# A two-layer hybrid decoder on one core: transposing attention probabilities six units behind their scores instead of four, with the second embedding kept in DRAM

## The chip, the cores and the metric

The kernel runs on one core of one Trainium2 chip. The metric is the device time of an execution in microseconds (us). Before the change the median of three runs is 1397.23 us, the lowest 1396.04, the highest 1397.76.

## What is computed

A decoder of two layers over 512 tokens of width 1024. Layer 0 mixes by retention and mLSTM heads, layer 1 by sparse attention with 16 query heads in two groups; in both a gated MLP with a short convolution and a gated input embedding follow. The change lies in layer 1: its attention, and the embedding that is computed beside the attention and used in the MLP behind it.

```
def reference(...):                                    # layer i = 1
    h = h + nsa_mixer(rms_norm(h, nsa_norm_g), ...)    # sparse attention
    h = h + conv_ffn(rms_norm(h, ffn_norm_g[i]), ...)  # gelu(conv(a)) * b, then down
    e = rms_norm(p[i] @ ple_w[i], ple_norm_g[i])       # the input embedding
    gate = sigmoid(rms_norm(h, ple_gate_norm_g[i]) @ ple_w_gate[i])
    h = h + gate * e

# in nsa_mixer, for each block of 128 queries:
    s = einsum('bghqd,bgnd->bghqn', qq, kc) * scale    # compressed keys: 31 of them
    p_c = softmax(where(cvalid, s, NEG));  o_cmp = p_c @ vc
    ...                                                # selected and window branch:
    p_s = softmax(where(smask, s, NEG));   o_slc = p_s @ vg
    p_w = softmax(where(wmask, s, NEG));   o_win = p_w @ vwb
    return g[..., 0:1] * o_cmp + g[..., 1:2] * o_slc + g[..., 2:3] * o_win
```

With 512 tokens all eight blocks of 64 are selected and the window of 512 covers everything, so both branches are causal attention over all keys, each with its own keys and values.

## The kernel before

Activations lie transposed, features on the partitions and the 512 tokens along the free axis. Each large product runs as three matmuls of split numbers (`mm3`, L152 to L154): high times high, high times low, low times high. A weight tile of 512 KB is loaded by SP (`load`, L146), copied to its high half by ACT (L133) and its remainder made by DVE or POOL (L134; `lo_seq` says which of the two); three tiles are in flight.

**Attention.** The work is cut in 96 units, six for each head: `UNITS` names the query block j (3, 1, 2, 0) and the branches b of each unit. The blocks j = 3 and j = 2 are too wide for both branches in a PSUM bank and take two units, the others one. A loop written out by hand (L1046 and on, `for step in range(...)`) does in each step: `scores` of unit `step`; `probs` of unit `step - LAG`; the hooks of that step; `values` of the heads that are due. The `values` of half a head come `VALUES_LAG` steps behind the last transposes that they read.

- `scores` (L889 to L910): two matmuls of queries with keys (L899, L900) and one that adds the causal mask (L901), into one of four PSUM banks "a"; DVE takes the negative maximum (L902), ACT the exponential with its sum (L904). When both branches of a block are there, DVE takes the reciprocal of the sums (L907) and POOL multiplies each branch by reciprocal and gate (L909), in place. The exponential goes to a tile "pr" of 128 x 512, of which there are six.
- `probs` (L912 to L923): PE transposes the gated probabilities in blocks of 128 x 128 (L921) into one of three PSUM banks "b"; ACT and DVE split them into high (L133) and low half (L134), tiles "pt".
- `values` (L925 and on): the products with the compressed values (L931, L932) and with the values (L943) into the one bank "o"; ACT (L947), DVE (L951) and POOL (L134) add and split the head's result.

**Hooks.** Beside the units, at steps given in `START`, stand the eight steps of the embedding (steps 1 to 8), the norm of the second group's queries (L818 to L831, steps 6 and 14), their transposes (L838, from 20), the second group's compressed scores and probabilities (L858 to L880, steps 42 and 47), the fetch of four blocks of the residual that had been kept in DRAM (L103, step 51), and the eight pieces of the first half of the output projection (`out_piece`, steps 60 to 74). The second half of the projection follows the loop and ends with L277.

**The embedding** (`Embed`, from L1116 on). `step(m)` computes rows 128 m and on, and ACT copies them out of PSUM (L1132) to where `place(m)` says. For layer 1 that is a tile of the pool "y", 28 tiles of 128 x 512 that also hold the split normed input, the split queries, the compressed probabilities and the split head outputs. `later(i)` is called in the MLP behind each pair of up products: it squares and sums the eight tiles, then scales them.

The program's order is the order of priority; a scheduler puts the instructions on each engine and gives out the tiles, and weight loads carry a priority 500 instructions ahead (`AHEAD`). So on PE transposes of one unit stand between scores of others. Each engine, SP's queue of DMAs too, works through its own list in order.

Of the kernel before, what the change touches and what calls it, by code (L numbers as in the profile page):

```python
# [10 lines left out]
F32 = mybir.dt.float32  # L11
# [8 lines left out]
P = 128  # L20
T = 512
NTT = T // P
D = 1024
KD = D // P
# [5 lines left out]
OFF = (0, 512, 1024, 896)  # L30
SPAN = 1280
WARM = 10
LAG, VALUES_LAG = 4, 2
UNITS = ((3, (0,)), (3, (1,)), (1, (0, 1)), (2, (0,)), (2, (1,)), (0, (0, 1)))
START = {"embed": (1, 1), "q_norm": (6, 8), "q_stack": (20, 6), "cmp_scores": 42, "cmp_probs": 47, "fetch": 51, "out": (60, 2)}
BANKS = {"a": 4, "b": 3, "o": 1}
# [15 lines left out]
class Norm:  # L52
    def __init__(self):
        self.h, self.l = [], []


class Rows(list):
    pass


class Trunk:
# [553 lines left out]
    def nsa_mixer(self):  # L615
        nc, I, tc = self.nc, self.I, self.tc
# [3 lines left out]
        with ExitStack() as ctx:  # L620
            np_ = ctx.enter_context(tc.tile_pool(name="nsa", bufs=1))
# [262 lines left out]
                return pc  # L884


            parts = []

            def scores(hd, j, bs):  # L889
                g, nb = hd // 8, len(bs)  # L890
                w = (j + 1) * P
                qt, br = qs[hd][:, j * P : w], slice(bs[0], bs[-1] + 1)
                nmx = np_.tile([P, nb], F32, name=self.nm("nmx"), tag=f"sm{nb}", bufs=4)
                if bs[0] == 0:
                    parts.append([np_.tile([P, 2], F32, name=self.nm("sm"), tag="sums", bufs=4), []])
                sm, prs = parts[-1]
                pr = np_.tile([P, T], F32, name=self.nm("pr"), tag="pr", bufs=6)[:, 0 : nb * w].rearrange("p (b s) -> p b s", b=nb)
                s = self.ps("a")[:, 0 : nb * w].rearrange("p (b s) -> p b s", b=nb)
                nc.tensor.matmul(s, qt, kst[0][g][:, br, 0:w], start=True, stop=False)  # L899
                nc.tensor.matmul(s, qt, kst[1][g][:, br, 0:w], start=False, stop=False)  # L900
                nc.tensor.matmul(s[:, :, j * P : w], identb, maskb.unsqueeze(1).to_broadcast([P, nb, P]), start=False, stop=True)  # L901
                nc.vector.tensor_reduce(nmx, s, AX, ALU.max, negate=True)  # L902
                for b in range(nb):
                    nc.scalar.activation(pr[:, b], s[:, b], AF.Exp, bias=nmx[:, b : b + 1], accum_out=sm[:, bs[b] : bs[b] + 1])  # L904
                    prs.append(pr[:, b])
                if bs[-1] == 1:
                    nc.vector.reciprocal(sm, sm)  # L907
                    for b in range(2):
                        nc.gpsimd.tensor_scalar(prs[b], prs[b], sm[:, b : b + 1], gate[:, j, hd, 1 + b : 2 + b], ALU.mult, ALU.mult)  # L909
                return pr  # L910
# [93 lines left out]
            def piece(half, m):  # L1004
                return lambda: self.out_piece(I["w_nso"], half, m, *outs[half])

            emb = self.Embed(self, 1, lambda m: self.y().bitcast(F32))

            def embed(m):
                def run():  # L1010
# [54 lines left out]
    def ffn(self, i, e):  # L1065
        nc, I, tc = self.nc, self.I, self.tc
        with ExitStack() as ctx:
# [4 lines left out]
            def mm_up(f):  # L1072
                self.cycle = ("a", "b")
                return self.ws(I["w_up"][i, f], n), self.ws(I["w_up"][i, NF + f], n)
# [25 lines left out]
                    nc.vector.tensor_tensor(self.h[m], self.h[m], ps, ALU.add)  # L1100

            first = mm_up(0)
            self.norm_scale(n)
            act_up(0, *first)
            part = 0
# [8 lines left out]


    class Embed:  # L1116
        def __init__(self, trunk, i, place):
            self.k, self.i, self.place = trunk, i, place
            self.n, self.e = Norm(), []

        def step(self, m):
            tr, nc = self.k, self.k.nc
            if m == 0:
                self.p = [x.rearrange("p (k t) -> p k t", k=2) for x in tr.load(tr.I["pT"][self.i])]
            if m % 4 == 0:
                self.w = tr.load(tr.I["w_ple"][self.i, m // 4])
            ps = tr.bank()
            for k in range(2):
                s = slice(((m % 4) * 2 + k) * P, ((m % 4) * 2 + k + 1) * P)
                tr.mm3(ps, self.w[0][:, s], self.w[1][:, s], self.p[0][:, k], self.p[1][:, k], k == 0, k == 1)  # L1130
            e = self.place(m)
            nc.scalar.activation(e, ps, AF.Copy)  # L1132
            self.e.append(e)

        def later(self, i):
            tr = self.k
            if i < KD:
                tr.acc_square(self.n, i, self.e[i])
            elif i == KD:
                tr.norm_scale(self.n)  # L1140
            elif i <= 2 * KD:
                e = self.e[i - KD - 1]
                tr.nc.gpsimd.tensor_tensor(e, e, self.n.b, ALU.mult)
# [138 lines left out]
```

## Time and profile before

| | |
|---|---|
| median of three runs | 1397.23 us |
| the profiled execution, its own time | 1398.08 us |
| its span, first to last instruction | 1396.3 us |
| PE busy | 1369.7 us, 98% |
| DVE busy | 850.2 us, 61% |
| ACT busy | 638.8 us, 46% |
| POOL busy | 348.8 us, 25% |
| read from HBM, written | 122.60 MB, 3.15 MB |

The profile is of one execution. An engine counts as busy while an instruction of its own runs; waiting and issuing are not busy. Matmuls overlap and their ends are modelled, so a short pause of PE can hide behind the end of the matmul before it. The attention of layer 1 goes from about 764 us to 966 us; there DVE and ACT are far busier than in the mean over the span.

### The profile page before, as it was taken

How to read it: one execution, taken by the hardware profiler on the slowest of the kernel's cores; microseconds unless marked ns; L12 is line 12 of the kernel's file. 1: busy time of each engine (PE TensorE's matmuls, PEld its weight loads, DVE VectorE, ACT ScalarE, POOL GpSimd, SP SyncE). 2: the span in 40 equal slices, each digit the busy share in tenths (PEclk: the TensorE clock that was granted, in tenths of full speed). 3: DMA queues.
4: the chain of work that ended last, by engine and by line, in shares of the span. 5: the costliest groups of instructions: out<-in, count | busy, mean ns of one | idle time of the engine just before them, and what ended most of it. 6: DMA issues, size and time to landing. Idle time of an engine off the chain costs nothing.

```text
span 1396.3 us, 17997 instructions
## 1 busy us (share of the span) xinstructions
PE 1369.7 (98%) x6726; PEld 1123.2 (80%) x6726; DVE 850.2 (61%) x1382; ACT 638.8 (46%) x1121; POOL 348.8 (25%) x347
## 2 busy tenths in 40 slices
PE   9999999999999999999999899999999999999998
PEld 7778778888888888887788677777888888888887
DVE  6665656666356434566857898776566346534555
ACT  5257426444124323454455787676444223313441
POOL 4466101132031101122110765544122023100120
PEclk9999999999999999999999999999999999999999
DMA  6433323232323323233343100010233323333232
GB/s 216 123 113 105 107 77 104 91 106 91 106 85 98 105 91 97 84 124 103 107 143 98 46 1 31 29 33 21 87 105 94 102 76 108 104 91 102 80 106 76
DMA packets 40031, 127.96 MB, mean 92 GB/s; under 512 B 4740, under 2 KB 5380, under 8 KB 39944
## 3 DMA queue, kind: packets, MB, share of 16 engines
q1 hardware_dynamic: 39656, 126.68, 29.4%
q8 instruction: 53, 0.87, 0.3%
q14 instruction: 34, 0.28, 0.1%
q10 hardware_dynamic: 288, 0.14, 0.0%
HBM read 122.60 MB, written 3.15 MB: 90 GB/s over the span
## 4 chain that ended last, share of the span: by engine, by line
PE 82%; DVE 4%; issue 4%; ACT 4%; POOL 2%; DMA 0%; POOLq 0%; DVEq 0%; ACTq 0%
PE ps L152 25%; PE ps L153 25%; PE ps L154 25%; PE ps L943 2%; PE ps L921 1%; ACT pr L904 1%; DVE nmx L902 1%; ACT pt L133 1%; DVE wl L134 1%; PE ps L363 1%; DVE pt L134 1%; PE ps L899 1%; PE ps L900 1%; PE ps L421 1%; POOL acc L200 1%
## 5 line engine op out<-in xcount | busy, mean ns | idle before, releaser
L152 PE MATMUL ps<-y,wh 128*128 128x512 f32 (+1 forms) x1112 | 434.4, 391 | 1.7 <-ACT rb L239 1.1
L153 PE MATMUL ps<-y,wh 128*128 128x512 f32 (+1 forms) x1112 | 431.6, 388 | 0.6 <-POOL y L134 0.6
L154 PE MATMUL ps<-y,wl 128*128 128x512 f32 (+1 forms) x1112 | 431.2, 388 | 0.0
L133 ACT ACTIVATE wh<-wr 128x1024 fp32r<-128x1024 f32 (+2 forms) x223 | 230.3, 1036 | 418.0 <-PE ps L153 344.8
L134 DVE TENSOR_TENSOR wl<-wr,wh 128x1024 fp32r<-128x1024 f32 (+2 forms) x199 | 244.9, 1233 | 43.2 <-ACT wh L133 42.2
L152 PEld LDWEIGHTS ps<-y,wh 128*128 128x128 f32 x1112 | 209.0, 188 | 45.5 <-ACT rb L239 1.3
L153 PEld LDWEIGHTS ps<-y,wh 128*128 128x128 f32 x1112 | 209.0, 188 | 43.6 <-POOL y L134 1.1
L154 PEld LDWEIGHTS ps<-y,wl 128*128 128x128 f32 x1112 | 208.8, 188 | 43.3 <-DVE wl L134 0.2
L1085 POOL TENSOR_TENSOR sc<-sc,rb 128x512 f32<-128x512 f32 x44 | 56.9, 1294 | 474.3 <-ACT sc L1084 468.5
L200 POOL TENSOR_TENSOR acc<-acc,sc 128x512 f32<-128x512 f32 x48 | 73.1, 1524 | 261.0 <-ACT sc L198 258.1
L152 PE MATMUL ps<-gh,wh 128*128 128x512 f32 x352 | 136.9, 389 | 0.0
L153 PE MATMUL ps<-gl,wh 128*128 128x512 f32 x352 | 136.9, 389 | 0.0
L154 PE MATMUL ps<-gh,wl 128*128 128x512 f32 x352 | 136.9, 389 | 0.0
L1100 DVE TENSOR_TENSOR hp<-hp,ps 128x512 f32<-128x512 f32 x48 | 33.0, 688 | 130.4 <-PE ps L154 130.4
L909 POOL TENSOR_SCALAR pr<-pr,sm,gate 128x512 f32<-128x512 f32 (+3 forms) x128 | 77.6, 620 | 64.8 <-DVE sm L907 54.2
L1086 DVE TENSOR_TENSOR sc<-ps,sc 128x512 f32<-128x512 f32 x44 | 30.4, 692 | 92.5 <-POOL sc L1085 85.6
L1078 DVE TENSOR_TENSOR a<-ps,rb 128x512 f32<-128x512 f32 x44 | 30.4, 690 | 91.9 <-PE ps L154 89.1
L152 PEld LDWEIGHTS ps<-gh,wh 128*128 128x128 f32 x352 | 66.1, 188 | 13.7
L153 PEld LDWEIGHTS ps<-gl,wh 128*128 128x128 f32 x352 | 66.1, 188 | 13.7
L154 PEld LDWEIGHTS ps<-gh,wl 128*128 128x128 f32 x352 | 66.1, 188 | 13.7
L1084 ACT ACTIVATE sc<-sc 128x512 f32<-128x512 f32 x44 | 27.8, 632 | 101.1 <-DVE sc L1083 101.1
L904 ACT ACTIVATE pr<-ps,nmx 128x512 f32<-128x512 f32 (+3 forms) x128 | 67.2, 533 | 9.4 <-DVE nmx L902 6.0
(284 smaller groups left out, 2006.8 us busy)
## 6 DMA issues: line engine op xcount, KB each, us to landing
wr<-in_w_up_dram SPq DMA_DIRECT2D x88, 512.0 KB, 3.6
wr<-in_w_down_dram SPq DMA_DIRECT2D x32, 512.0 KB, 3.6
wr<-in_w_plg_dram SPq DMA_DIRECT2D x16, 512.0 KB, 3.6
wr<-in_w_down_dram SPq DMA_DIRECT2D x16, 384.0 KB, 3.1
hp<-in_xT_dram SPq DMA_DIRECT2D x16, 256.0 KB, 4.2
wr<-in_w_abo_dram SPq DMA_DIRECT2D x8, 512.0 KB, 3.7
wr<-in_w_dram SPq DMA_DIRECT2D x8, 512.0 KB, 3.6
wr<-in_w_q_dram SPq DMA_DIRECT2D x8, 512.0 KB, 3.7
```

Source lines behind the costliest of these rows:

```text
L133: self.nc.scalar.activation(hi, src, AF.Copy)
L134: (eng or self.nc.vector).tensor_tensor(lo, src, hi.bitcast(F32), ALU.subtract)
L152: mm(out, ah, bh, start=first, stop=False)
L153: mm(out, ah, bl, start=False, stop=False)
L154: mm(out, al, bh, start=False, stop=last)
L200: eng.tensor_tensor(n.acc, n.acc, sq, ALU.add)
L904: nc.scalar.activation(pr[:, b], s[:, b], AF.Exp, bias=nmx[:, b : b + 1], accum_out=sm[:, bs[b] : bs[b] + 1])
L909: nc.gpsimd.tensor_scalar(prs[b], prs[b], sm[:, b : b + 1], gate[:, j, hd, 1 + b : 2 + b], ALU.mult, ALU.mult)
L1078: nc.vector.tensor_tensor(a, pa, n.b, ALU.mult)
L1085: nc.gpsimd.tensor_tensor(c, c, n.b, ALU.mult)
L1086: nc.vector.tensor_tensor(c, pb, c, ALU.mult)
L1100: nc.vector.tensor_tensor(self.h[m], self.h[m], ps, ALU.add)
```

## The change

`LAG` becomes 6. A unit's transposes are then issued behind the scores of the unit six steps later, and six tiles of sums are kept instead of four. Nine tiles hold probabilities instead of six: of three units in a row two take a tile "pr", the third one takes a tile "y". The eight tiles of the second embedding no longer lie in "y" during attention: `step` copies each to a tile of "sc" (six tiles of 128 x 512 for short-lived values) and stores it to DRAM from SP, and `back`, called in the MLP behind the first pair of up products, takes eight tiles "y" and loads them again. For layer 0 nothing is stored or loaded, since `away` is None there. The class `Rows`, which nothing used, goes.

```diff
--- before.py
+++ after.py
@@ -30,7 +30,7 @@
 OFF = (0, 512, 1024, 896)
 SPAN = 1280
 WARM = 10
-LAG, VALUES_LAG = 4, 2
+LAG, VALUES_LAG = 6, 2
 UNITS = ((3, (0,)), (3, (1,)), (1, (0, 1)), (2, (0,)), (2, (1,)), (0, (0, 1)))
 START = {"embed": (1, 1), "q_norm": (6, 8), "q_stack": (20, 6), "cmp_scores": 42, "cmp_probs": 47, "fetch": 51, "out": (60, 2)}
 BANKS = {"a": 4, "b": 3, "o": 1}
@@ -52,10 +52,6 @@
 class Norm:
     def __init__(self):
         self.h, self.l = [], []
-
-
-class Rows(list):
-    pass
 
 
 class Trunk:
@@ -884,7 +880,7 @@
                 return pc
 
 
-            parts = []
+            parts, turn = [], [0]
 
             def scores(hd, j, bs):
                 g, nb = hd // 8, len(bs)
@@ -892,9 +888,11 @@
                 qt, br = qs[hd][:, j * P : w], slice(bs[0], bs[-1] + 1)
                 nmx = np_.tile([P, nb], F32, name=self.nm("nmx"), tag=f"sm{nb}", bufs=4)
                 if bs[0] == 0:
-                    parts.append([np_.tile([P, 2], F32, name=self.nm("sm"), tag="sums", bufs=4), []])
+                    parts.append([np_.tile([P, 2], F32, name=self.nm("sm"), tag="sums", bufs=6), []])
                 sm, prs = parts[-1]
-                pr = np_.tile([P, T], F32, name=self.nm("pr"), tag="pr", bufs=6)[:, 0 : nb * w].rearrange("p (b s) -> p b s", b=nb)
+                turn[0] = (turn[0] + 1) % 3
+                pr = np_.tile([P, T], F32, name=self.nm("pr"), tag="pr", bufs=6) if turn[0] else self.y().bitcast(F32)
+                pr = pr[:, 0 : nb * w].rearrange("p (b s) -> p b s", b=nb)
                 s = self.ps("a")[:, 0 : nb * w].rearrange("p (b s) -> p b s", b=nb)
                 nc.tensor.matmul(s, qt, kst[0][g][:, br, 0:w], start=True, stop=False)
                 nc.tensor.matmul(s, qt, kst[1][g][:, br, 0:w], start=False, stop=False)
@@ -1004,7 +1002,7 @@
             def piece(half, m):
                 return lambda: self.out_piece(I["w_nso"], half, m, *outs[half])
 
-            emb = self.Embed(self, 1, lambda m: self.y().bitcast(F32))
+            emb = self.Embed(self, 1, lambda m: self.sc(), self.dram.tile([D, T], F32, name="emb"))
 
             def embed(m):
                 def run():
@@ -1100,6 +1098,7 @@
                     nc.vector.tensor_tensor(self.h[m], self.h[m], ps, ALU.add)
 
             first = mm_up(0)
+            e.back()
             self.norm_scale(n)
             act_up(0, *first)
             part = 0
@@ -1114,8 +1113,8 @@
 
 
     class Embed:
-        def __init__(self, trunk, i, place):
-            self.k, self.i, self.place = trunk, i, place
+        def __init__(self, trunk, i, place, away=None):
+            self.k, self.i, self.place, self.away = trunk, i, place, away
             self.n, self.e = Norm(), []
 
         def step(self, m):
@@ -1130,7 +1129,17 @@
                 tr.mm3(ps, self.w[0][:, s], self.w[1][:, s], self.p[0][:, k], self.p[1][:, k], k == 0, k == 1)
             e = self.place(m)
             nc.scalar.activation(e, ps, AF.Copy)
+            if self.away is not None:
+                nc.sync.dma_start(self.away[m * P : (m + 1) * P], e)
             self.e.append(e)
+
+
+        def back(self):
+            tr = self.k
+            if self.away is not None:
+                self.e = [tr.y().bitcast(F32) for _ in range(KD)]
+                for m in range(KD):
+                    tr.nc.sync.dma_start(self.e[m], self.away[m * P : (m + 1) * P])
 
         def later(self, i):
             tr = self.k
```

## Rows read from the trace of the kernel before

**Rows 1.** The page, part 1 (busy time of each engine, share of the span, instructions).
```profile
PE 1369.7 (98%) x6726; PEld 1123.2 (80%) x6726; DVE 850.2 (61%) x1382; ACT 638.8 (46%) x1121; POOL 348.8 (25%) x347
```

**Rows 2.** Busy time of each engine in two stretches: the attention of layer 1, and the last output pieces with the first up products behind them. Columns: the stretch in us from the span's start, its length, busy us (and instructions) of PE, PE's weight loads, DVE, ACT, POOL; granted clock of PE as a share of full speed; busy share of the DMA engines; GB/s.
```profile
764.00:966.00 202.00, 187.93 (x1260) 149.33 (x1260) 159.86 (x387) 151.11 (x442) 110.53 (x153) 0.98 0.08 25
966.00:1008.00 42.00, 42.00 (x192) 34.66 (x191) 24.03 (x40) 21.69 (x30) 10.39 (x7) 1.00 0.25 76
```

**Rows 3.** The timeline around the start of head 14 (columns: start in us, us, engine, line, operation, out<-in, count; in brackets the engine's idle time before it and what ended it). First transposes alone and four in a row, then the chain from the second exponential of the unit j=3 to the split of its first half.
```profile
936.20 0.27 PE L921 MATMUL ps<-ident,pr 128*128 128x128 f32 x1
...
936.91 0.60 PE L921 MATMUL ps<-ident,pr 128*128 128x128 f32 x4
...
941.79 0.69 ACT L904 ACTIVATE pr<-ps,nmx 128x512 f32<-128x512 f32 x1
...
942.68 0.17 DVE L907 RECIPROCAL sm<-sm 128x2 f32<-128x2 f32 x1
...
943.01 2.06 POOL L909 TENSOR_SCALAR pr<-pr,sm,gate 128x512 f32<-128x512 f32 x3 [2.86 <-DVE sm L907]
...
943.84 0.66 PE L921 MATMUL ps<-ident,pr 128*128 128x128 f32 x4 [0.27 <-POOL pr L909]
...
944.53 0.60 ACT L133 ACTIVATE pt<-ps 128x512 fp32r<-128x512 f32 x1
```

**Rows 4.** Busy time by head, columns as in rows 2; a head is counted from its first exponential to that of the next one. In this order heads 2, 7, 8, 13 and 14.
```profile
797.35:808.75 11.40, 9.68 (x72) 7.52 (x71) 10.67 (x32) 8.28 (x28) 9.02 (x13) 1.00 0.31 93
848.50:865.15 16.65, 14.16 (x104) 11.10 (x103) 15.06 (x39) 11.03 (x31) 10.57 (x14) 1.00 0.19 63
865.15:873.92 8.77, 7.93 (x62) 6.76 (x63) 7.78 (x20) 7.75 (x27) 4.32 (x7) 1.00 0.01 3
930.55:939.79 9.24, 8.66 (x67) 6.87 (x65) 7.78 (x20) 8.29 (x28) 6.07 (x10) 1.00 0.00 1
939.79:948.59 8.80, 8.53 (x67) 6.81 (x65) 7.50 (x20) 7.93 (x27) 4.78 (x9) 1.00 0.01 2
```

**Rows 5.** Who waited for whom on PE in attention: us in total, times, the longest in us.
```profile
PE ps L921 <- DVE pt L134: 3.4, 7, 1.1
PE ps L921 <- POOL pr L909: 3.2, 4, 1.5
PE ps L880 <- POOL sc L870: 2.6, 2, 2.3
PE ps L921 <- DVE sm L907: 1.3, 3, 0.4
```

**Rows 6.** The timeline of POOL around 800 us, and the transposes that end the wait; columns as in rows 3.
```profile
794.33 4.75 POOL L134 TENSOR_TENSOR wl<-wr,wh 128x1024 fp32r<-128x1024 f32 x2
...
799.89 2.06 POOL L818 TENSOR_TENSOR sc<-ep 128x512 f32<-128x512 f32 x2
...
801.91 1.54 POOL L909 TENSOR_SCALAR pr<-pr,sm,gate 128x512 f32<-128x512 f32 x2
...
802.75 0.44 PE L921 MATMUL ps<-ident,pr 128*128 128x128 f32 x2 [1.52 <-POOL pr L909]
```

**Rows 7.** Groups of instructions in attention (764 to 966 us): line, engine, operation, out<-in, one of the shapes, count; busy us, mean ns of one; idle us of the engine before them and what ended most of it. In this order the gating, the exponentials, DVE's half of the split, ACT's half.
```profile
L909 POOL TENSOR_SCALAR pr<-pr,sm,gate 128x512 f32<-128x512 f32 (+3 forms) x128 | 77.6, 620 | 64.8 <-DVE sm L907 54.2 <-PE ps L943 3.0 <-PE ps L838 2.9
L904 ACT ACTIVATE pr<-ps,nmx 128x512 f32<-128x512 f32 (+3 forms) x128 | 67.2, 533 | 9.4 <-DVE nmx L902 6.0 <-DVE sm L907 2.4 <-DVE tiny L188 0.4
L134 DVE TENSOR_TENSOR pt<-ps,pt 128x256 fp32r<-128x256 f32 (+3 forms) x128 | 60.3, 483 | 16.9 <-ACT pt L133 15.0 <-PE ps L943 1.0 <-issue 0.2
...
L133 ACT ACTIVATE pt<-ps 128x256 fp32r<-128x256 f32 (+3 forms) x128 | 54.1, 441 | 27.4 <-PE ps L921 23.5 <-PE ps L943 3.1 <-PE ps L858 0.4
```

**Rows 8.** The timeline of SP's queue in three short windows, columns as in rows 3: two weight loads for the output projection, and four in a row for the up products (time from the first issue to the end of the fourth, 0.33 us each to issue).
```profile
781.63 0.33 SPq L146 DMA_DIRECT2D wr<-in_w_nso_dram  x1
...
796.76 0.33 SPq L146 DMA_DIRECT2D wr<-in_w_nso_dram  x1
...
1032.57 15.65 SPq L146 DMA_DIRECT2D wr<-in_w_up_dram  x4
```

**Rows 9.** Three short stretches, columns as in rows 2: the last two before the first transposes of attention, and one at its end.
```profile
755.00:760.00 5.00, 4.95 (x45) 4.66 (x44) 4.33 (x9) 3.95 (x7) 0.00 (x0) 1.00 0.31 104
760.00:765.00 5.00, 5.00 (x21) 4.11 (x21) 4.08 (x10) 1.41 (x3) 1.05 (x1) 0.55 0.02 6
955.00:965.00 10.00, 9.83 (x66) 7.81 (x64) 5.04 (x13) 5.21 (x14) 2.09 (x4) 1.00 0.01 2
```

**Rows 10.** The copies of both embeddings out of PSUM, ACT L1132: count, shortest, median and longest in ns, first and last start in us; the line of embedding 1.
```profile
L1132 ACT ACTIVATE y<-ps x8: 580/600/637, 767.0 to 790.8; 128x512 f32<-128x512 f32 x8
```

**Rows 11.** DMA issues from 640 to 1080 us: out<-in, engine, operation, count, KB of each, median us from issue to landing.
```profile
wr<-in_w_up_dram SPq DMA_DIRECT2D x18, 512.0 KB, 3.6
...
hp<-keep SPq DMA_DIRECT2D x4, 256.0 KB, 4.0
keep<-hp SPq DMA_DIRECT2D x2, 256.0 KB, 2.5
```

**Rows 12.** What SP's queue waited for from 740 to 860 us: us in total, times, the longest in us.
```profile
SPq L103 <- PE ps L900: 56.8, 1, 56.8
SPq L146 <- POOL wl L134: 41.0, 3, 24.3
```

**Rows 13.** The additions of the output pieces to the residual, DVE L277, from 900 to 1010 us; columns as in rows 10.
```profile
L277 DVE TENSOR_TENSOR hp<-hp,ps x13: 681/687/689, 902.5 to 984.4; 128x512 f32<-128x512 f32 x13
```

## The prediction

> **What bounds the kernel now.** I read the page first: TensorE (PE) is busy for 98% of the span [rows 1]. Then the stretches: the sparse attention of layer 1 (764 to 966 us) has PE busy 187.93 of 202.00 us, the projection and the up products behind it 42.00 of 42.00 [rows 2]. So only attention has time to give: 14.1 us of shown idle. The matmul row hides some of each wait: a transpose is busy 0.27 us, four in a row 0.60 us [rows 3], so the next starts 0.11 us after the last one and a wait shows about 0.16 us too short. The Trainium skill (Perfetto Trace Analysis, Identifying the Most-Contended Engine) says that matmul busy time is no measure of TensorE's headroom and that the share of weight loads is; by that, with 149.33/202.00 here against 34.66/42.00 behind, the headroom would be an estimated 21 us instead of 14.1. It is a ceiling only; no term below uses it.
>
> Head by head: one head of plain attention lasts 8.77 to 9.24 us, with ACT busy 7.75 to 8.29 and DVE 7.50 to 7.78 [rows 4]. ACT is nearly as full as PE: bubbles of 0.9 to 1.0 us a head are all that ACT leaves. Heads 2 and 7 carry the second query group's norm and the second compressed softmax, and there DVE is the full one: 10.67 of 11.40 and 15.06 of 16.65.
>
> Who ends PE's waits in attention: its transposes L921 wait 3.2 us (4 times) for POOL's gating L909, 1.3 us (3 times) with the reciprocal L907 as the last releaser, which is the same wait one step earlier, and 3.4 us (7 times) for DVE's split L134, that is for a free PSUM bank "b"; L880 waits 2.6 us for the softmax of the compressed scores [rows 5]. At a head's start one sees why the gating is late [rows 3]: the second half of unit j=3 starts its exponential at 941.79, the reciprocal runs at 942.68, POOL gates both halves from 943.01, and at 943.84 PE, idle 0.27 us, starts the transposes of the first half; ACT's split follows at 944.53. Unit j=3 has two scores steps and the reciprocal needs both, so its first half is transposed only three steps after the scores that release it, not four.
>
> **The change, step by step.** (1) *Six units of distance instead of four.* Each gating gets two more units, that is two sixths of a head: 2/6 x 8.8 = 2.9 us. The seven gating waits are at most 1.5 us long, so all of them should go: 4.5 us shown + 7 x 0.16 hidden = 5.6 us. From this I take two things back. The longest wait (1.52 us at 802.75, hidden part included 1.7) comes after POOL spent 4.75 us on two weight remainders and 2.06 us on squares before it reached the gating [rows 6]; it lies in head 2, where DVE has 11.40 - 10.67 = 0.7 us to give, so 1.0 us of it stays. And where gating is no longer late, the next late thing is bank "b": ACT's split waits for transposes 23.5 us in all, DVE's split for ACT's 15.0 us [rows 7], and PE's waits for that bank are 0.5 us each. I let three of the six remaining waits turn into such a one: 1.5 us. Left: 5.6 - 1.0 - 1.5 = 3.1 us. Bounds: 0 (all come back at the bank) and 5.6.
>
> (2) *Start and end.* Two units of scores move ahead of the first transposes. At the start PE sits idle 2.3 us in one wait before L880, and more work is there to fill it. A score matmul takes 0.21 us from start to start (a weight tile of 24 of them every 15.32/3 = 5.1 us [rows 8]), two units about 1.0 us. At the end PE is busy 9.83 of 10.00 us [rows 9], so work taken from there counts in full. I take 0.9 us, between 0 and the 2.6 us of L880.
>
> (3) *Probability tiles.* Every third unit's tile comes from the pool "y" instead of "pr", so nine tiles serve distance six where six served distance four. The operations are the same on the same shapes: 128 exponentials of 533 ns, 128 gatings of 620 ns. The exponentials' idle time is put down to DVE alone, none of it to PE's transposes, which would mean a missing tile [rows 7], and the eight "y" tiles that embedding 1 held pay for the three lent. Nothing; if a tile came late, the cost is in rival B.
>
> (4) *Embedding 1 to DRAM.* The eight ACT copies L1132 stay (600 ns, 767.0 to 790.8 [rows 10]) but go to the six-deep pool "sc", and eight stores of 256 KB are issued on SP. A like store lands in 2.5 us [rows 11], its issue takes SP 0.33 us [rows 8], 2.6 us in all, on a queue that sleeps here: 41.0 us behind POOL's weight remainders, 56.8 us before L103 [rows 12]. Taken at nothing, as long as a store doesn't sit behind such a sleeping load; bounds 0 to 9 us (rival C).
>
> (5) *Embedding 1 back.* Eight loads of 256 KB behind the first up product. Like loads (hp<-keep, four together) land in 4.0 us [rows 11], so eight take some 8 us of transfer; DMA is 0.25 busy there [rows 2]. SP carries them between weight loads. Weights run three tiles ahead: 3 x 5.1 - 3.6 to land = 11.7 us of cover. The first is needed by the square behind the second pair of up products, some 20 us after the start. Taken at nothing; bounds 0 to 14 us (rival D).
>
> (6) *Sums tiles, hooks.* The sums pool grows with the distance; the hooks keep their step numbers. The output pieces at step 60 now find head 7 done at step 55 instead of 53: five steps, over 7 us. Nothing.
>
> Sum: 3.1 + 0.9 = 4.0 us. The profiled execution took 1398.08 us (span 1396.3), so it would become 1394.1; the median of the runs shown is 0.85 us lower, so I predict 1393.2 us. A measurement of this kernel tells about 0.2% (2.8 us) from no change: faster ends at 1394.4, slower begins at 1400.0.
>
> **Rivals.** *A, more than the waits.* With gating out of the way the plain heads close up to ACT's own time: 0.9 us in each of eight (5, 6, 8, 9, 13 to 15 and half of 2 and 7) is 7.2, with 2.6 at the start 9.8 us: 1387.4. For it: ACT has the room in every plain head. Against: DVE and the bank take turns with ACT within a head. 0.17.
> *B, the wait moves to the bank.* "b" has three banks whatever the distance; transposes that are ready earlier only wait there, or for lent tiles. Then the start's 0.9 us is left: 1396.3. For it: bank waits are as long as POOL's [rows 5], and heads 2 and 7 are full on DVE [rows 4]. Against: at the head's start it is the gating that releases. 0.20, no difference.
> *C, a sleeping load holds the stores; slower.* SP works in order. It sleeps up to 24.3 us before a weight load L146 that waits for POOL [rows 12]; such loads went out at 781.63 and 796.76 [rows 8]. If the stores stand behind the second, the six tiles of "sc" are all held when the last copy comes at 790.8 [rows 10]; it waits until 796.76 + 0.33 + 2.5 = 799.6, and ACT stops for 9 us with exponentials and splits behind it. 1393.2 + 9 = 1402. It decides as soon as six stores are issued after 796.76. Against: even the last copy would be done 5 us before that load goes out. 0.13.
> *D, the way back; slower.* If the loads stand on SP before weights while they wait for "y" tiles that the output projection reads until 984.4 [rows 13], weights stop for up to 18 us from 966 on and come behind 8 us of transfers, against 11.7 us of cover: 18 + 8 - 11.7 = 14 us at worst, 7 in the middle: 1400.2. 0.08.
> *E, the clock.* From 760 to 765, behind 5 us of 45 short matmuls, PE was granted 0.55 of its clock, so the 1.2 GHz level for most of it; from 955 to 965, with many transposes, 1.00, the 2.4 GHz level [rows 9]. A start with other work in it, or an end with two more units of transposes and no scores, could lose that level once more: 5 x 0.45 = 2.3 us at least, 1395.5 or more. The Trainium skill (TensorE: Matmul & The Clock Gate, Part 4) says that transposes don't count as busy for that gate; by that the end with two more units of them is where the clock would fall. The end of the trace speaks against it, with 1.00. 0.06, no difference.
>
> **How the numbers follow.** The forecast has 0.36 (1390 to 1394.4), A 0.17, B 0.20, C 0.13, D 0.08, E 0.06. Faster: 0.36 + 0.17 = 0.53; same: 0.26; slower: 0.21. The range goes from 1387 (A) to 1402 (the middle of C and D); outside lie what goes beyond A and the worse halves of C and D, under 0.2. The forecast's own range is 1390 to 1394.4.
>
> **What would show it.** Right: no wait of L921 for POOL L909 or DVE L907 between 785 and 960; plain heads at 8.2 to 8.6 us with ACT busy nearly throughout; PE full from 966 on. Wrong: the same total under L921 <- DVE L134 (B); ACT L1132 or L947 idle before a DMA of the embedding (C); PE idle or squares late in the first 40 us of the last FFN, SP waiting before the loads (D); a granted clock under 1.00 after 785 (E). What would make the prediction wrong most is the order of instructions on each engine: it comes out new for the whole stretch, and rows of before don't show it.

## The result, and the profile after

The changed kernel takes 1405.58 us (median of 6 runs, 1403.17 to 1407.27) against 1396.63 us before on the same chip: ratio 1.0063, 95% interval 1.0053 to 1.0074. It is **slower by 8.9 us**; the forecast was 1393.2 us. The profiled execution took 1406.34 us, its span is 1404.6.

The page of after, part 1, against [rows 1]:
```profile
PE 1376.8 (98%) x6726; PEld 1128.9 (80%) x6726; DVE 847.9 (60%) x1382; ACT 638.4 (45%) x1121; POOL 349.3 (25%) x347
```
The same instructions keep TensorE (PE) busy 7.1 us longer. The stretches of after (columns as in [rows 2]; the first two answer to it, 8.3 us later at their end):
```profile
764.00:974.30 210.30, 195.88 (x1265) 155.56 (x1265) 163.38 (x390) 150.85 (x443) 113.36 (x156) 0.94 0.10 34
974.30:1016.30 42.00, 42.00 (x192) 34.70 (x191) 24.05 (x41) 21.74 (x30) 10.38 (x7) 1.00 0.37 126
...
785.00:805.00 20.00, 15.32 (x91) 11.80 (x90) 17.28 (x42) 13.20 (x40) 13.03 (x15) 0.91 0.37 130
805.00:825.00 20.00, 15.91 (x84) 11.45 (x85) 14.77 (x46) 13.61 (x45) 11.18 (x15) 0.76 0.01 1
```
The same two stretches of the kernel before:
```profile
785.00:805.00 20.00, 16.92 (x118) 13.19 (x118) 16.07 (x40) 16.53 (x49) 16.13 (x19) 1.00 0.18 54
805.00:825.00 20.00, 18.57 (x132) 14.40 (x131) 18.64 (x53) 17.87 (x57) 13.69 (x19) 1.00 0.01 1
```
Nothing is lost behind attention: from its last split to the end of the span both traces have 435.1 us (961.20 to 1396.3, 969.49 to 1404.6). Not all of the 8.3 us between these two executions arises in attention, though. The sums of the first query norm of layer 1, which stand ahead of everything that was changed, start 2.3 us later already (before, then after; columns as in [rows 10]):
```profile
L819 DVE TENSOR_REDUCE tiny<-sc x8: 621/671/686, 729.7 to 802.0; 128x8 f32<-128x512 f32 x8
L815 DVE TENSOR_REDUCE tiny<-sc x8: 668/678/686, 732.0 to 807.0; 128x8 f32<-128x512 f32 x8
```
Of this 1.0 us is there within the first 20 us of the span, and most of the rest came where the clock fell for 3.4 us at 85 us: from 84 to 89 us the granted clock was 0.66 after and 1.00 before. The profiled executions of e1, e3, e6 and e16 have that fall too, those of the other runs don't, and e16 has neither the lag nor the storage of the change. So about 6 of the 8.3 us are attention's.

Within attention the loss arises between 785 and 825: 175 matmuls there instead of 250, and a granted clock of 0.91 and 0.76 instead of 1.00, which is time at the 1.2 GHz level. Counted by the n-th matmul, the changed kernel is 11.5 us behind by then (the 3801st starts at 813.3 us before and at 824.7 after), and it regains 3.2 us by the end of attention.

What PE waited for in the attention of after, against [rows 5] (L919 are the transposes, L907 the gating, L905 the reciprocal):
```profile
PE ps L919 <- DVE pt L130: 5.6, 9, 1.7
PE ps L876 <- POOL sc L866: 2.3, 1, 2.3
PE ps L919 <- DVE tiny L183: 2.1, 1, 2.1
...
PE ps L919 <- POOL pr L907: 0.3, 1, 0.3
PE ps L919 <- DVE sm L905: 0.2, 1, 0.2
```
The gating waits are gone as forecast, 4.5 us down to 0.5. New is a wait for a "tiny" operation: L179 to L184 are the reciprocal square root of the query norm, a chain of small operations on VectorE (DVE). The timeline of GpSimd (POOL) of after around it (columns as in [rows 3]):
```profile
779.68 2.40 POOL L130 TENSOR_TENSOR wl<-wr,wh 128x1024 fp32r<-128x1024 f32 x1 [1.10 <-ACT wh L129]
...
782.92 2.03 POOL L814 TENSOR_TENSOR sc<-ep 128x512 f32<-128x512 f32 x2
...
788.35 2.37 POOL L130 TENSOR_TENSOR wl<-wr,wh 128x1024 fp32r<-128x1024 f32 x1 [0.98 <-ACT wh L129]
791.26 2.36 POOL L130 TENSOR_TENSOR wl<-wr,wh 128x1024 fp32r<-128x1024 f32 x1 [0.54 <-ACT wh L129]
795.85 2.04 POOL L821 TENSOR_TENSOR ep<-ep,tiny 128x512 f32<-128x512 f32 x2 [2.24 <-DVE tiny L818]
```
The squares of the first norm (L814; here and below that of the second group's queries) run at 782.92. Before, they ran at 750.59, ahead of the softmax of the compressed scores:
```profile
750.59 2.27 POOL L818 TENSOR_TENSOR sc<-ep 128x512 f32<-128x512 f32 x2 [36.45 <-ACT ep L811]
```
VectorE, PE and ACT around 790 us of after:
```profile
788.25 0.17 DVE L184 SCALAR_TENSOR_TENSOR tiny<-tiny,tiny 128x16 f32<-128x16 f32 x1
788.46 2.29 DVE L182 TENSOR_TENSOR tiny<-tiny 128x16 f32<-128x16 f32 x1
...
791.14 0.16 DVE L183 SCALAR_TENSOR_TENSOR tiny<-tiny,tiny 128x16 f32<-128x16 f32 x1
791.22 0.41 DVE L130 TENSOR_TENSOR pt<-ps,pt 128x256 fp32r<-128x256 f32 x1
791.56 2.09 DVE L184 SCALAR_TENSOR_TENSOR tiny<-tiny,tiny 128x16 f32<-128x16 f32 x1
...
791.78 0.30 PE L919 MATMUL ps<-ident,y 128*128 128x128 f32 x1 [1.71 <-DVE pt L130]
...
794.81 0.94 PE L919 MATMUL ps<-ident,pr 128*128 128x128 f32 x4 [2.08 <-DVE tiny L183]
...
796.85 0.60 ACT L129 ACTIVATE pt<-ps 128x512 fp32r<-128x512 f32 x1 [4.46 <-PE ps L941]
797.35 1.33 ACT L826 ACTIVATE y<-ep 128x256 fp32r<-128x256 f32 x4
798.57 0.46 ACT L902 ACTIVATE y<-ps,nmx 128x256 f32<-128x256 f32 x1
```
Read down: two operations of 16 columns take 2.29 and 2.09 us instead of 0.17, each until a weight remainder on GpSimd ends (790.72, 793.62). The splits that free PSUM bank "b" stand behind them on VectorE, so PE waits 1.71 and 2.08 us. ACT waits 4.46 us for the values, then takes the norm's own splits (L826), which needed L821 of GpSimd. Only then come the exponentials: none starts between 784.35 and 798.57.

The parts forecast at nothing: the copies out of PSUM, against [rows 10], and the read-back (count, shortest, median and longest in ns, first and last start).
```profile
L1131 ACT ACTIVATE sc<-ps x8: 578/597/616, 768.0 to 788.5; 128x512 f32<-128x512 f32 x8
...
L1142 SPq DMA_DIRECT2D y<-emb x8: 382/384/430, 989.8 to 1001.7; - x8
```
The transfers, against [rows 11]:
```profile
emb<-sc SPq DMA_DIRECT2D x8, 256.0 KB, 2.0
y<-emb SPq DMA_DIRECT2D x8, 256.0 KB, 4.2
```
The stores land 2.0 us after issue in the median; the read-back is in by 1001.7 + 0.4 + 4.2 = 1006.3. Neither shows in a wait of PE.

### The profile page after: what moved, and what is told of

Same layout as the page of the kernel before. It is cut to its first block, busy times and chain, and to the rows that moved or that the text cites. A ratio compares the mean times of both kernels' runs of the same rounds, so it can differ in the third digit from the quotient of the medians.

```text
span 1404.6 us, 17997 instructions
## 1 busy us (share of the span) xinstructions
PE 1376.8 (98%) x6726; PEld 1128.9 (80%) x6726; DVE 847.9 (60%) x1382; ACT 638.4 (45%) x1121; POOL 349.3 (25%) x347
## 4 chain that ended last, share of the span: by engine, by line
PE 83%; DVE 5%; issue 4%; POOL 2%; ACT 2%; DMA 0%; POOLq 0%; ACTq 0%; DVEq 0%
PE ps L148 25%; PE ps L149 25%; PE ps L150 24%; PE ps L941 2%; PE ps L919 2%; PE ps L897 1%; DVE pt L130 1%; PE ps L898 1%; DVE nmx L900 1%; DVE wl L130 1%; PE ps L359 1%; PE ps L417 1%; POOL acc L196 1%; ACT wh L129 0%; ACT pt L129 0%
## 5 line engine op out<-in xcount | busy, mean ns | idle before, releaser
L130 POOL TENSOR_TENSOR wl<-wr,wh 128x1024 fp32r<-128x1024 f32 x22 | 53.6, 2439 | 67.7 <-ACT wh L129 60.2
L129 ACT ACTIVATE pt<-ps 128x256 fp32r<-128x256 f32 (+3 forms) x128 | 54.3, 446 | 34.7 <-PE ps L919 21.4
```

The costliest lines, as they stand in the source:

```text
L129: self.nc.scalar.activation(hi, src, AF.Copy)
L130: (eng or self.nc.vector).tensor_tensor(lo, src, hi.bitcast(F32), ALU.subtract)
```

## The experiments

Each ratio is to the kernel before on the same chip in the same session (before: medians 1396.6 to 1397.9). **T x c** is the mean over the runs of time times mean granted clock, a measure of the schedule with the clock taken out. For one and the same kernel this is fair: 35 runs of the kernel before go from 1399.5 us at clock 0.994 to 1393.5 at 0.998, 6.0 us for 0.004, and 0.004 of the span is 5.6 us. Between kernels it is an assumption: it counts half of the time at 1.2 GHz as lost, also where PE waits in it. By it some 2 us of the loss are the schedule's (1392.9 against 1391) and some 6 the clock's (0.9912 against 0.9955).

| run | lag | embedding, lent tiles | squares early | remainders | us | ratio (95%) | clock | T x c |
|---|---|---|---|---|---|---|---|---|
| before | 4 | SBUF, no | - | GpSimd | 1396.6 to 1397.9 | 1 | 0.9955 | 1391 |
| after | 6 | DRAM, yes | - | GpSimd | 1405.58 | 1.0063 (1.0053 to 1.0074) | 0.9912 | 1392.9 |
| e1 | 4 | DRAM, yes | - | GpSimd | 1405.81 | 1.0066 (1.0053 to 1.0078) | 0.9934 | 1397.1 |
| e2 | 6 | SBUF, 7 own | - | GpSimd | 1400.09 | 1.0021 (1.0012 to 1.0030) | 0.9935 | 1391.1 |
| e3 | 4 | DRAM, no | - | GpSimd | 1400.60 | 1.0022 (1.0011 to 1.0033) | 0.9950 | 1393.4 |
| e4 | 6 | DRAM, yes | - | VectorE | 1402.97 | 1.0038 (1.0026 to 1.0050) | 0.9920 | 1391.2 |
| e5 | 6 | DRAM, yes | first | GpSimd | 1399.26 | 1.0027 (1.0015 to 1.0039) | 0.9936 | 1390.9 |
| e6 | 4 | DRAM, yes | first | GpSimd | 1399.26 | 1.0015 (1.0005 to 1.0024) | 0.9961 | 1393.7 |
| e7 | 4 | SBUF, no | - | GpSimd | 1395.09 | 0.9982 (0.9973 to 0.9991) | 0.9975 | 1391.0 |
| e8 | 6 | DRAM from "y", yes | - | GpSimd | 1400.72 | 1.0030 (1.0019 to 1.0041) | 0.9929 | 1390.9 |
| e9 | 6 | DRAM, yes | both | GpSimd | 1397.69 | 1.0006 (0.9996 to 1.0015) | 0.9929 | 1388.1 |
| e10 | 4 | SBUF, no | late | GpSimd | 1400.85 | 1.0028 (1.0015 to 1.0041) | 0.9949 | 1394.4 |
| e11 | 6 | DRAM, yes | first | VectorE | 1397.70 | 1.0002 (0.9992 to 1.0012) | 0.9936 | 1388.8 |
| e12 | 4 | SBUF, no | both | GpSimd | 1394.59 | 0.9981 (0.9972 to 0.9989) | 0.9967 | 1390.4 |
| e13 | 6 | SBUF, 7 own | both | GpSimd | 1403.03 | 1.0033 (1.0020 to 1.0046) | 0.9916 | 1390.2 |
| e14 | 4 | DRAM, yes | both | GpSimd | 1400.52 | 1.0029 (1.0020 to 1.0038) | 0.9935 | 1391.8 |
| e15 | 6 | DRAM, yes | both | VectorE | 1395.38 | 0.9989 (0.9980 to 0.9999) | 0.9942 | 1386.9 |
| e16 | 4 | SBUF, no | both | VectorE | 1395.00 | 0.9984 (0.9975 to 0.9992) | 0.9966 | 1390.2 |
| e17 | 4 | DRAM, yes | both | VectorE | 1402.46 | 1.0037 (1.0025 to 1.0050) | 0.9922 | 1391.4 |
| e18 | 5 | DRAM, yes | both | VectorE | 1395.86 | 0.9986 (0.9977 to 0.9995) | 0.9951 | 1388.5 |

**Which part costs: e1 to e4.** Theory S: storage makes the first norm late. Theory O: the order of the lag of six.
```
e1: LAG 6 -> 4                       (on the changed kernel)
e2: LAG 4 -> 6, pr bufs 6 -> 7, sums bufs 4 -> 6   (on the kernel before)
e3: e1, and pr always from its own six tiles
e4: the changed kernel without "if m == 4: self.lo_seq = 'g'"
```


> The changed kernel with the transposes four units behind the scores again; the embedding still goes to DRAM through the six general tiles and every third score unit is still lent an embedding tile. Theory S (storage: the embedding's copies take the general tiles which the first query norm of the second group needs, its chain of small operations starts some 10 us late and falls among GpSimd's weight remainders, which hold VectorE's small operations; TensorE starves and its clock halves): the loss stays, 1404 to 1407 us, with half-clock stretches between 790 and 830 us. Theory O (order: with six units of lag ScalarE's exponentials stand queued behind splits that wait for values, and the store has nothing to do with it): the loss goes, 1396 to 1399 us, and TensorE at full clock from 780 us on.

> The kernel before with the lag of six alone: seven own probability tiles (all that fits) and six tiles of sums, embedding in its eight tiles until the FFN. Theory S: no loss, 1392 to 1397 us, the gating waits of the attention (5.6 us of them before) gone, the copies at 767 to 791 us as before. Theory O: 1403 to 1407 us, a stretch without exponentials of 10 us or more before 800 us and some 10 us at half clock after it.

> The kernel before with the embedding alone moved: copied into general tiles, stored to DRAM, read back in the FFN; the lag is four and no tile is lent. Theory S: 1403 to 1407 us, the query norm's small operations after 785 us as in the changed kernel. Theory O: 1396 to 1399 us. If this is at 1397 and the first of the four at 1405, lending the tiles would be the cause, which neither theory has.

> The changed kernel with the remainders of the attention's later weight tiles left on VectorE instead of going to GpSimd after the fifth embedding step. Theory S: VectorE's small operations are held no more (0.17 us each instead of 2.1 to 2.3), the lull at 791 to 798 us is gone, 1397 to 1400 us; VectorE has four more 1024-column operations to do, some 1.2 us each. Theory O: no change beyond those, 1403 to 1408 us.

At a lag of four the loss stays whole (e1), so the order that a lag of six brings is not its cause. DRAM alone costs 3.1 us (e3), where S had 6 to 10; lending, which neither theory had, adds 6.1. PE's longest wait in e1, and what VectorE did meanwhile:
```profile
794.93 0.47 PE L919 MATMUL ps<-ident,y 128*128 128x128 f32 x1 [4.30 <-DVE pt L130]
...
790.44 1.94 DVE L182 TENSOR_TENSOR tiny<-tiny 128x16 f32<-128x16 f32 x1
...
792.77 1.91 DVE L183 SCALAR_TENSOR_TENSOR tiny<-tiny,tiny 128x16 f32<-128x16 f32 x1
```
In e1, as in after, two remainders fall into the norm's chain, in e3 one (2.34 us). e4 takes them off GpSimd: no small operation is held, 3.5 us of 8.9 come back (ratio 1.0063 to 1.0038), but the squares are still late (782.34) and the time is 3 us above the range of S. e2, the lag of six alone, loses 2.9 us: neither theory had that. In its trace the longest wait of PE is at the second norm, with the clock falling at 801.9 for 6.8 us:
```profile
802.83 0.45 PE L921 MATMUL ps<-ident,pr 128*128 128x128 f32 x1 [3.19 <-DVE tiny L820]
```
The same wait comes up again in e5.

**The late squares: e5, e6, e8, e10, e7.**
```
e5: squares of the first norm issued in hook 0, their sums and the rest left in hook 6
    hooks[0] = [lambda: early.append(q_squares(zq[0], nc.gpsimd))]
e6: e5 with LAG 4
e8: emb = self.Embed(self, 1, lambda m: self.y().bitcast(F32), self.dram.tile(...))
e10: kernel before; the squares' tile is one that unit 3's probabilities hold first
e7: kernel before; START["q_norm"] (6, 8) -> (9, 5)
```


> The changed kernel, its lag of six, DRAM and lent tiles kept, with one thing moved: the two squares of the first query norm of the second group take their general tiles in step 0, ahead of the embedding's copies; the rest of that norm stays in step 6. Theory S (the copies push the norm's squares from 751 to 783 us, and its small operations among GpSimd's remainders): squares at 750 to 752 us again, the norm's products done by 788 us instead of 798, and 1397 to 1401 us, what the lag of six alone gave being 1400.1. Rival R (lending, stores or the lag cost it and the late norm is only carried along): 1403 to 1407 us with the squares early all the same.

> The same early squares with the lag back at four: the embedding in DRAM and the lent tiles alone, without the late norm. Theory S: 1395 to 1399 us, nothing left of the 8 us that this kernel lost without the early squares. Rival R: 1403 to 1407 us.

> The changed kernel with the embedding's copies stored from the pool of 28 tiles in which the kernel before kept them, instead of from the six general tiles; the lag of six, the DRAM copy and the lent tiles stay. Theory S: the squares are back at 751 us, 1397 to 1401 us. Rival R: 1403 to 1407 us.

> The kernel before, its lag, its storage and its hooks kept; only the tile of the first norm's squares is made to come free late: it is one extra tile that holds the third score unit's probabilities first, so that the squares stand behind that unit's transposes, near 783 us instead of 751. Theory S: lateness alone costs 3 to 8 us, 1400 to 1406 us, the norm's products done near 796 us and its small operations held by remainders. Rival R: 1396 to 1399 us.

> The kernel before with its first query norm put into step 9 instead of step 6 (the second stays in step 14): the embedding stays in its tiles, nothing is lent or stored, the lag is four. Its squares now stand behind the softmax of the compressed scores and a weight remainder on GpSimd. Theory S: squares at 780 us or later, products done at 794 us or later, and the loss without any of the change, 1400 to 1406 us. Rival R: 1396 to 1399 us.

With the squares' tiles claimed ahead of the copies the squares run early again in e5:
```profile
750.71 2.14 POOL L813 TENSOR_TENSOR sc<-ep 128x512 f32<-128x512 f32 x2 [36.66 <-ACT ep L807]
```
Of the loss 5.0 us (1.0063 to 1.0027) come back at a lag of six, 7.1 us (1.0066 to 1.0015) at four, where the time is 0.3 us above the range of S. Copies that leave the general tiles alone do the same (e8: squares at 749.78, 4.6 us back). The reverse holds: late squares in the kernel before, with no DRAM and nothing lent, cost 3.9 us (e10). Its chain, on GpSimd, VectorE and PE:
```profile
781.44 1.03 POOL L821 TENSOR_TENSOR late<-ep 128x512 f32<-128x512 f32 x1
...
787.06 2.39 POOL L134 TENSOR_TENSOR wl<-wr,wh 128x1024 fp32r<-128x1024 f32 x1
...
791.39 2.33 POOL L134 TENSOR_TENSOR wl<-wr,wh 128x1024 fp32r<-128x1024 f32 x1
...
787.26 2.22 DVE L187 SCALAR_TENSOR_TENSOR tiny<-tiny,tiny 128x16 f32<-128x16 f32 x1
...
791.47 2.28 DVE L825 TENSOR_SCALAR tiny<-tiny 128x16 f32<-128x16 f32 x1
...
797.16 0.79 PE L904 MATMUL ps<-hp,y 128*128 128x512 f32 x1 [5.39 <-DVE y L834]
```
PE's scores wait 5.39 us there, until the norm's last split (L834). So S is shown both ways for this term, some 5 of the 8.9 us: early squares give them back, late ones bring most of them into the kernel before. e7 tested nothing of it, since its squares ran at 750.74 all the same: a later hook does not make them later on GpSimd. It came out 2.5 us faster than before with the rest of attention reordered, which says how much a new order alone can move. In T x c it equals the kernel before (1391.0), so its gain is all clock.

**What holds the lag of six back: e9, e11, e12.** In e5 the gating waits of L925 (here the transposes) are gone and one long wait has come, ahead of a stretch at half clock that begins at 800.0. GpSimd, VectorE and PE in e5:
```profile
790.25 4.74 POOL L130 TENSOR_TENSOR wl<-wr,wh 128x1024 fp32r<-128x1024 f32 x2
794.97 1.52 POOL L913 TENSOR_SCALAR pr<-pr,sm,gate 128x512 f32<-128x512 f32 x2
796.45 2.04 POOL L813 TENSOR_TENSOR sc<-ep 128x512 f32<-128x512 f32 x2
...
797.52 0.69 DVE L821 TENSOR_REDUCE tiny<-sc 128x8 f32<-128x512 f32 x1 [2.99 <-POOL sc L813]
...
799.68 0.30 PE L925 MATMUL ps<-ident,y 128*128 128x128 f32 x1 [3.33 <-DVE tiny L822]
```
VectorE stands 2.99 us at the second norm's sums, because its squares come behind two remainders; the next split stands behind the sums, and PE behind that split. It is the place of [rows 6].
```
e9:  e5, and the second norm's squares in hook 9 instead of 14
e11: e5, and the remainders on VectorE
e12: the kernel before with both pairs early (hooks 0 and 9)
```


> The changed kernel with the squares of both query norms ahead: the first pair in step 0, the second in step 9 instead of step 14, so that on GpSimd they stand ahead of the two weight remainders (4.8 us) instead of behind them. Theory W (the gating waits that the lag of six removed come back as one wait: VectorE stands at the second norm's sums until GpSimd has done remainders and squares, the transposes wait 3.4 to 3.8 us for the splits queued behind, and TensorE's clock halves for 6.8 us right after): no wait over 1.5 us between 795 and 805 us, no half-clock stretch there, 1393 to 1397 us. Rival V (the lag of six brings the half-clock stretches near 800 and 851 us whatever the second norm does): 1398 to 1401 us, as with the first pair alone (1399.3).

> The changed kernel with the first pair of squares in step 0 and the attention's later weight remainders on VectorE instead of GpSimd. Theory W: the second squares no longer stand behind 4.8 us of remainders, the wait of 3.6 us before 800 us falls under 1.5 us and its half-clock stretch goes; VectorE has four more 1024-column operations of some 1.2 us; 1394 to 1398 us. Rival V: 1398 to 1402 us.

> The kernel before, lag of four and its storage kept, with the same two pairs of early squares. Theory W: the wait of 1.7 us for GpSimd near 803 us shrinks to under 1 us, 1394 to 1397 us. Rival V: 1396 to 1398.5 us, no difference, since at a lag of four no half-clock stretch follows that wait.

Both edits bring the changed kernel level with the kernel before (1.0006, 1.0002), about 3 us each. e11 is as W said: PE's longest wait near 800 is 1.2 us there, and the clock falls only at 809.6. e9 misses W's range by 0.7 us and its signs too: a remainder held the chain again (2.29 us), PE waited 2.2 us for it, and the clock fell at 802.1 for 3.4 us. e12 is 2.7 us faster than before, as W had it.

**What the lag itself is worth: e13 to e18.** Here the forecast's term (theory P) stands against the lag giving nothing (theory Q).
```
e13: e2 with both pairs early          e14: e9 with LAG 4
e15: e9 with the remainders on VectorE  e16: e12 with the remainders on VectorE
e17: e15 with LAG 4                     e18: e15 with LAG 5
```


> The kernel before with the lag of six (seven own probability tiles, six tiles of sums) and both pairs of squares early; the embedding stays in SBUF. Against it stands the same with a lag of four (1394.6). Theory P (the forecast's own term holds once the norms are out of the way): 1391 to 1393 us. Theory Q (the lag of six gives nothing: what the gating waits held comes back as waits for VectorE's splits and as half-clock stretches of 3.4 to 6.8 us near 800 and 850): 1395 to 1399 us, mean clock under 0.995.

> The changed kernel with both pairs of squares early and the lag back at four; DRAM and lent tiles stay. Against it stands the lag of six with the same storage (1397.7) and the lag of four without the storage (1394.6). Theory P: 1399 to 1402 us, the lag of six being worth 2 to 4 us over it. Theory Q: 1394 to 1398 us, storage costing 0 to 3 us and the lag nothing.

> The changed kernel, lag of six and all its storage, with both pairs of squares early and the later weight remainders on VectorE: nothing of GpSimd's long operations holds the norms. Theory P: 1390 to 1394 us. Theory Q: 1395 to 1398 us with half-clock stretches at 800 to 860 us all the same.

> The kernel before, lag of four and its own storage, with both pairs of squares early and the later weight remainders on VectorE. Both theories: 1391 to 1395 us, no later than the same with the remainders on GpSimd (1394.6); over 1396 would say that VectorE's four more operations of 1.2 us cost more than the held small operations did.

> The changed kernel with both pairs of squares early and the weight remainders on VectorE, and the lag back at four: against the same with the lag of six (1395.4 us, time times mean clock 1386.9) only the lag differs. Theory P (the lag gives its 3 to 4 us once nothing long on GpSimd disturbs): 1398 to 1400 us. Theory Q (what the lag gives at full clock, 3 to 4 us in the product of time and mean clock, is given back as time at half clock): the product at 1390 to 1391, but the time at 1394.5 to 1397 us with a mean clock of 0.996 or more.

> The same with a lag of five. Theory P: between the two, 1396 to 1398 us. Theory Q: 1394 to 1397 us, product near 1388.5, mean clock between those of four and six.

e15 and e17 differ in the lag alone, with the weight remainders gone from GpSimd in this stretch: 0.9989 against 1.0037, so the lag of six is worth 6.7 us there, 4.5 us of it in T x c (1386.9 against 1391.4). A lag of five (e18, 0.9986) is worth as much, so the step from four to five gives it all in these kernels; its time lies in Q's range and 0.1 us under P's. e9 against e14 gives 3.2 us, but e5 against e6 1.7 us the other way. So Q, by which the lag gives nothing, is out for e15 and e17. P met its range in e14, but both kernels of the pair are slower than it said: 1395.4 for 1390 to 1394 in e15, 1402.5 for 1398 to 1400 in e17.

And e16, with neither the lag nor its storage, is as fast as e15: DRAM and lent tiles cost 7.4 us at a lag of four (e17 against e16), which the lag buys back. With seven own tiles instead, the lag gives a loss (e13 against e12, 7.3 us), beyond both theories. In T x c the two are level (1390.2, 1390.4), so the loss is one of clock. Two remainders hold the second norm's small operations in e13 (1.81 and 2.27 us), PE waits 2.9 us for the split behind them, and the clock falls at 802.4 for 10.2 us. The scores also wait 4.3 us for exponentials; whether seven tiles are too few for a distance of six was not tried.

PE's waits from 785 to 960 us, first e15, then e17:
```profile
PE ps L925 <- DVE pt L130: 3.0, 8, 0.9
PE ps L935 <- DVE sc L955: 1.6, 1, 1.6
```
```profile
PE ps L925 <- DVE pt L130: 5.2, 8, 3.3
PE ps L903 <- ACT y L908: 2.8, 1, 2.8
PE ps L925 <- POOL pr L913: 1.5, 3, 0.9
PE ps L925 <- DVE sm L911: 1.3, 3, 0.4
```
The gating waits L913 and L911 are e17's alone, 2.8 us; the rest of its loss is in two long waits that are not gating, and what of them is the lag's and what comes of the new order is not settled.

No version with the lag of six is better than the kernel before by more than those without it: e12, e7, e16, e18 and e15 lie between 0.9981 and 0.9989, inside one another's intervals. The simplest of them is e7, which changes two numbers of `START` (1395.1 us).

## Why the prediction was wrong

**Step 4 failed.** It took the embedding's way to DRAM at nothing "as long as a store doesn't sit behind such a sleeping load". It looked at SP's queue and left out who else uses the six tiles of "sc": the copies of steps 1 to 6 claim one each ahead of the norm's squares, which had run at 750.59 with nothing in their way. The squares moved to 782.92. That costs about 5 us of the 8.9 (5.0 in e5, 4.6 in e8), and lateness by itself costs 3.9 (e10). In the changed kernel the larger part of this is a lower clock (0.9912, 0.9936 in e5), for which the sum had no term; in e10 it is schedule (T x c 1394.4 against 1391).

Rival C named the right pool and nearly the right time (1402), but that was luck, for it had the wrong holder: a load that slept until 782.11 delayed two stores by 1.9 and 1.2 us, and ahead of its copies ACT stood idle for PE's products (5.1 us in all) and 0.2 us besides, not for a DMA.

**Step 1** was right in mechanism: the gating waits fell from 4.5 to 0.5 us. With step 2 it was put at 4.0 us; by T x c the schedule gave 4.2 (after against e1), 2.8 (e5, e6), 3.7 (e9, e14) and 4.5 us (e15, e17), but nothing with seven own tiles (e13, e12). In time it gave 0.4 us in the changed kernel (1.0066 to 1.0063), since the mean clock fell from 0.9934 to 0.9912, 3.1 us. **Step 2**: the long wait before L876 at the start (L880 before) stayed at 2.3 us.

**Step 3** was wrong as well: the lent tiles are in no wait for a tile, but the kernel with DRAM and lent tiles at a lag of four stands 6 us over DRAM alone (e1, e3). In e1 two remainders fall on the chain where e3 has one; why lending moves them there was not settled. It is no fixed price: at a lag of four DRAM and lent tiles together cost 2.1 us with the first squares early (e6), 4.8 with both pairs early (e14 against e12) and 7.4 with the remainders on VectorE as well (e17 against e16). DRAM without lending was not tried with early squares. **Steps 5 and 6** were right: 435.1 us in both, rival D out.

**Rival E** had the clock, at 0.06 and 2.3 us, but not where: beside the start, which spent 6.8 us at 1.2 GHz (before 10.2), three more stretches of the attention fell to that level, 17 us long together, at 795.0, 815.5 and 859.8. The first two, and the end of attention:
```profile
794.98:798.39 3.41, 3.41 (x19) 3.41 (x18) 1.83 (x7) 1.54 (x5) 2.04 (x2) 0.50 0.34 133
815.46:825.70 10.24, 8.25 (x33) 5.82 (x32) 5.85 (x16) 8.63 (x30) 6.76 (x9) 0.50 0.01 2
960.00:970.00 10.00, 9.47 (x76) 8.15 (x75) 7.14 (x20) 7.24 (x25) 4.38 (x7) 1.00 0.01 3
```
The first begins just after the two waits of 1.71 and 2.08 us. For the end of attention E named the Trainium skill (TensorE: Matmul & The Clock Gate, Part 4), by which transposes don't count as busy; the trace has 1.00 there (third row). Only 23 of its 76 matmuls are transposes, so the row doesn't test that sentence. Why the clock falls again near 850 us was not settled: it does so at a lag of six (e2, e5, e9, e15) and at a lag of four (e1, e14, e16, e17).

## What to carry to other kernels

Moving data "off the path" moves it through a pool: list who else claims that pool after it, and how early they ran. On an in-order engine a chain of small operations is as exposed as the longest operation of a neighbour that can hold it, so give such a chain its tiles and its slot first. When waits vanish and the time stays, compare time times clock: the gain may be there and lie under a lower clock. And compare the traces ahead of the change too: here 2.3 us of the difference between two executions lay in code that both kernels share.

## What the hardware showed

A VectorE operation on 16 columns that reads SBUF alone takes 0.17 us. When it starts while GpSimd makes a weight remainder (two inputs of 1024 columns, 2.4 us), it ends with that one (790.75 and 790.72 in after, 793.75 and 793.72 in e10): it took 0.8 us where little of the remainder was left (e12, from 779.79 to 780.57) and up to 2.4 us where all of it was. The kernel before has one such case already: 2.39 us at 779.24, until the remainder of 779.20 ends. Splits that read PSUM keep their time under a remainder (0.69 us at 795.75 in the kernel before, with a remainder from 794.33 to 796.74), and so do reciprocals of two columns (0.17 us at 796.45).

The Trainium skill (SBUF — State Buffer, Who interferes with whom) states this: with two SBUF inputs VectorE needs a port that GpSimd shares, whoever starts first keeps it for the whole instruction, and the other blocks. The traces agree. Operations with one input were held as well (2.28 us in e10, 2.29 in e9), so two inputs are not the whole condition. The forecast read [rows 6] for the gating alone and did not ask what those remainders would do to a chain of small operations beside them.
